# Masked softmax of a batched matmul: transfers of eight rows to a partition over four batches, in buffers of 2 MB

## Chip, cores and metric

One core of a Trainium2 chip. The metric is the time of one execution on the device in microseconds (us); lower is better. The kernel before takes 91.02 us (median of 3 runs, 90.93 to 91.16). Faster or slower means by over 2%.

## The reference

```python
batch, m, k, n = 16, 512, 512, 512            # x: (16, 512, 512), weight: (512, 512), float32
y = scale * np.matmul(x, weight)              # scale = 0.125
y = np.where(mask == 1, y, -1e9)              # mask: 1 strictly below the diagonal
y_exp = np.exp(y - np.max(y, axis=-1, keepdims=True))
return (y_exp / np.sum(y_exp, axis=-1, keepdims=True)).astype(np.float32)
```

16.8 MB come in as x, 16.8 MB go out. Row 0 of each batch is fully masked and becomes 1/512.

## The kernel before

Work goes in 16 units of 1 MB. A unit is one half of the rows (`h`) of two neighbouring batches: partition `2p + e` holds rows `4p` to `4p + 3` of that half of batch `e`, which are 8 KB in one run of memory. For the upper half only 256 columns are computed. The mask's diagonal blocks are turned into an additive `band`, which one extra matmul adds. All transfers go through one queue.

```python
X_BUFS = 8
OUT_BUFS = 8
T = 4
x_r = x.rearrange("(c e) (h p t) k -> c h p e (t k)", e=2, h=2, t=T)
out_r = out.rearrange("(c e) (h p t) n -> c h p e (t n)", e=2, h=2, t=T)
# ... cut: tiles
def load(u):
    xf = x_pool.tile([P, T, K], FP32, name="xf")
    seq(nc.sync.dma_start(xf.rearrange("p t k -> p (t k)"), x_r[u // 2, u % 2]))
# ... cut: cast (DVE), transpose (PE), evict (DVE and ACT), multiply (PE, exp on ACT), normalise (DVE)
load(0)
seq(nc.sync.dma_start(w_f32, weight.rearrange("(p kt) n -> p kt n", kt=KT)))
load(1)
seq(nc.sync.dma_start(diag_f32, diag_r))      # four 128 x 128 blocks of the mask, 512-byte pieces
for u in range(2, X_BUFS):
    load(u)
# ... cut: clears, spins that keep PE's clock up, first two units, band
for u in range(U + 1):
    if 2 <= u + 1 < U:
        transpose(u + 1)
    if u + 2 < U:
        cast(u + 2)
    if 2 <= u + 1 < U:
        evict(u + 1)
    if u < U:
        multiply(u)
    if u >= 1:
        normalise(u - 1)
        store(u - 1)
        if u - 1 + X_BUFS < U:
            load(u - 1 + X_BUFS)
```

The softmax here doesn't subtract the row's maximum and nothing guards it: scores larger than these inputs give would overflow.

## Time and profile before

| | before |
|---|---|
| time, span in the profile | 91.02 us, 89.1 us |
| DMA share of the queue | 94.2% |
| last store issued / landed | 80.1 / 88.05 us |
| PE busy | 74.3 us, ends at 77.3 us |

### The profile page before, as it was taken

Reading aid. Unit: us, or ns where it says so; the run is one execution under the profiler, and the core shown is the slowest. Engines: PE = TensorE matmul, PEld = TensorE weight load, DVE = VectorE, ACT = ScalarE, POOL = GpSimd, SP = SyncE. Lnnn points to the kernel's source line nnn. Section 1 sums busy time; section 2 is a strip of 40 time slices with the busy share of each in tenths; the row PEclk is TensorE's granted clock in tenths of the full one; section 3 lists DMA queues with packets and bytes.
Section 4 is the critical chain, followed back from the end, with each engine's and each line's share of the span. In section 5 each row is a group of like instructions: output and inputs, shape, how many; then the busy total and the mean of one; then the engine's idle time right before and its main releaser. Section 6 shows DMA issues by size and latency. Waiting matters only on the chain.

```text
span 89.1 us, 1666 instructions
## 1 busy us (share of the span) xinstructions
PE 74.3 (83%) x616; PEld 50.0 (56%) x616; DVE 60.3 (68%) x123; ACT 55.0 (62%) x154; POOL 7.3 (8%) x20
## 2 busy tenths in 40 slices
PE   4967979899999999999999999999999999700000
PEld 1315454685795598579659847964984784300000
DVE  5876263989499779949977977967494999080000
ACT  5402604977697686969768786977778796710000
POOL 7620000002001000200100020002000102000000
PEclk9999999999999999999999999999999999995555
DMA  1899779999999999999999999999999999999970
GB/s 22 313 408 431 293 289 438 419 431 419 427 419 431 419 431 419 416 419 431 423 427 412 434 427 423 423 431 423 419 416 445 416 427 419 434 419 427 434 316 33
DMA packets 5287, 34.97 MB, mean 393 GB/s; under 512 B 544, under 2 KB 1056, under 8 KB 1056
## 3 DMA queue, kind: packets, MB, share of 16 engines
q1 hardware_dynamic: 5280, 34.87, 94.2%
q8 instruction: 5, 0.08, 0.3%
q14 instruction: 2, 0.02, 0.0%
HBM read 18.09 MB, written 16.78 MB: 392 GB/s over the span
## 4 chain that ended last, share of the span: by engine, by line
PE 72%; DMA 10%; DVE 4%; SPq 1%; ACT 1%; DVEq 0%; issue 0%; ACTq 0%
PE py L117 47%; PE pt L93 15%; DMA xf<-in_x_dram 10%; PE py L126 8%; PE py L175 2%; DVE ot L153 1%; DVE xb L84 1%; SPq L79 1%; ACT ot L136 1%; SPq L163 1%; DVE band L226 0%; DVEq L272 0%; ACT band L226 0%; PE py L219 0%; DVE rinv L151 0%
## 5 line engine op out<-in xcount | busy, mean ns | idle before, releaser
L117 PE MATMUL py<-w_bf,xt 128*128 128x256 bf16 (+1 forms) x256 | 49.4, 326 | 0.3 <-ACT band L226 0.3
L136 ACT ACTIVATE ot<-py 128x256 f32<-128x256 f32 (+1 forms) x64 | 31.2, 493 | 7.3 <-PE py L126 7.1
L117 PEld LDWEIGHTS <-xt 128*128 128x128 bf16 x256 | 24.4, 98 | 12.6 <-issue 0.5
L104 ACT COPY xt<-pt 128x1024 bf16<-128x1024 bf16 x16 | 16.2, 1012 | 13.6 <-PE pt L93 9.4
L84 DVE CAST xb<-xf 128x2048 bf16<-128x2048 f32 x16 | 19.5, 1220 | 7.2 <-DMA xf<-in_x_dram 7.2
L153 DVE TENSOR_SCALAR ot<-ot,rinv 128x256 f32<-128x256 f32 (+1 forms) x64 | 23.5, 431 | 0.8
L93 PE MATMUL pt<-ident_bf,xb 128*128 128x128 bf16 x256 | 17.0, 219 | 1.7 <-DVE xb L84 1.7
L93 PEld LDWEIGHTS <-xb 128*128 128x128 bf16 x256 | 15.9, 114 | 3.6 <-DVE xb L84 2.7
L126 PE MATMUL py<-band,ident_bf 128*128 128x256 bf16 x64 | 17.4, 273 | 0.0
L103 DVE COPY xt<-pt 128x1024 bf16<-128x1024 bf16 x16 | 11.0, 686 | 6.4 <-PE pt L93 6.4
L136 ACT ACTIVATION_READ_ACCUMULATOR ot<-py 128x1 f32 x64 | 12.8, 200 | 0.0
L175 PE MATMUL py<-zeros 128*128 128x512 bf16 x36 | 10.3, 447 | 1.2 <-DVE zeros L170 1.2
L155 POOL MEMSET ot<- 2x256 f32 x8 | 3.6, 449 | 65.8 <-DVE ot L153 65.8
L126 PEld LDWEIGHTS <-ident_bf 128*128 128x128 bf16 x64 | 6.3, 98 | 4.1
L175 PEld LDWEIGHTS <-zeros 128*128 128x128 bf16 x36 | 3.9, 112 | 6.3 <-issue 2.7
L151 DVE RECIPROCAL rinv<-rsum 128x4 f32<-128x4 f32 x16 | 2.7, 168 | 2.6 <-ACT ot L136 2.6
L183 DVE MEMSET ot<- 128x1024 f32 x4 | 3.6, 912 | 0.6 <-issue 0.6
L226 DVE CAST band<-py 64x256 bf16<-64x256 f32 x4 | 1.4, 408 | 1.4 <-PE py L219 1.4
L226 ACT CAST band<-py 64x256 bf16<-64x256 f32 x4 | 1.4, 367 | 1.4 <-DVE band L226 1.4
L190 ACT ACT_TABLE_LOAD x1 | 1.3, 1283 | 0.7 <-PEq L258 0.7
L184 POOL MEMSET ot<- 2x256 f32 x4 | 1.2, 301 | 1.5 <-DVE ot L183 1.4
L190 ACT COPY spread<-ident_bf 128x128 bf16<-128x128 bf16 x4 | 1.0, 330 | 0.2 <-POOL ident_bf masks.py:199 0.2
(14 smaller groups left out, 6.7 us busy)
## 6 DMA issues: line engine op xcount, KB each, us to landing
xf<-in_x_dram SPq DMA_DIRECT2D x16, 1024.0 KB, 14.9
out_dram<-ot SPq DMA_DIRECT2D x16, 1024.0 KB, 12.1
w_f<-in_weight_dram SPq DMA_DIRECT2D x1, 1024.0 KB, 7.0
diag_f<-in_mask_dram SPq DMA_DIRECT2D x1, 256.0 KB, 10.5
```

The source lines that it names most:

```text
L84: seq(nc.vector.tensor_copy(xb, st_x.pop(u)))
L93: nc.tensor.transpose(st_pt[u][kt // 2][:, kt % 2, t], xb[:, t].rearrange("p (k kt) -> p kt k", kt=KT)[:, kt], ident_bf,)
L103: seq(nc.vector.tensor_copy(xt[:, 0:2], pt[0]))
L104: seq(nc.scalar.copy(xt[:, 2:4], pt[1]))
L117: nc.tensor.matmul(py[:, :NC], lhsT=xt[:, kt, t], rhs=w_bf[:, kt, :NC], start=(kt == 0), stop=(kt == KT - 1),)
L126: nc.tensor.matmul(py[:, h * HB : NC], lhsT=ident_bf, rhs=band[:, h, t], start=False, stop=True, skip_group_check=True,)
L136: nc.scalar.activation(out=ot[:, t, :NC], in_=py[:, :NC], func=AF.Exp, bias=0.0, scale=float(scale), accum_out=rsum[:, t : t + 1],)
L153: seq(nc.vector.tensor_scalar_mul(ot[:, t, :NC], ot[:, t, :NC], rinv[:, t : t + 1]))
L155: seq(nc.gpsimd.memset(ot[0:2, 0, :HB], 1.0 / N))
L175: seq(nc.tensor.matmul(idle, lhsT=zeros[:, :P], rhs=zeros, start=True, stop=True))
L183: nc.vector.memset(ots[i][:, :, HB:], 0.0)
L226: seq(copy(band[half, :, t, g * P : (g + 1) * P], src[half, :, g]))
```

## The change

The intent: longer runs, so fewer packets, and fewer and larger transfers. A transfer now covers half the rows of four batches, with eight rows (16 KB) to a partition, 2 MB in all. It holds two units. The first load and the last store stay halved. Five load buffers and four output buffers of 2 MB replace eight and eight of 1 MB. A position in a partition now stands for one of eight rows, so the band has eight slots.

```diff
-X_BUFS = 8
-OUT_BUFS = 8
+X_BUFS = 5
+OUT_BUFS = 4
...
-    xb_pool = ctx.enter_context(tc.tile_pool(name="xb", bufs=3))
-    xt_pool = ctx.enter_context(tc.tile_pool(name="xt", bufs=3))
+    xb_pool = ctx.enter_context(tc.tile_pool(name="xb", bufs=2))
+    xt_pool = ctx.enter_context(tc.tile_pool(name="xt", bufs=2))
...
-    x_r = x.rearrange("(c e) (h p t) k -> c h p e (t k)", e=2, h=2, t=T)
+    x_r = x.rearrange("(c e) (h p t) k -> c h p e (t k)", e=E, h=2, t=S)   # E = 4, S = 8
...
-    band = const.tile([P, 2, T, HB], BF16, name="band")
-    ots = [const.tile([P, T, N], FP32, name=f"ot{i}") for i in range(OUT_BUFS)]
+    band = const.tile([P, 2, S, HB], BF16, name="band")
+    ots = [const.tile([P, S, N], FP32, name=f"ot{i}") for i in range(OUT_BUFS)]
...
-    for t in range(T):
+    for t in range(S):
         pm = psum_y.tile([P, N], FP32, name="py")
...
             normalise(u - 1)
-            store(u - 1)
-            if u - 1 + X_BUFS < U:
-                load(u - 1 + X_BUFS)
+            g, second = divmod(u - 1, 2)
+            if g == G - 1:
+                store(g, slots(u - 1))
+            elif second:
+                store(g)
+                if g + X_BUFS < G:
+                    load(g + X_BUFS)
```

Look at the end: a store and the load behind it used to be issued for each unit, so the queue turned from stores to loads and back in steps of 1 MB. Now the steps are 2 MB.

More of the change, by code (lines that the diff above doesn't have):

```diff
@@ L43 @@
     K2, N = weight.shape
-    assert K == K2 and N == 512 and K == 512 and M == 512 and B % 2 == 0
+    assert K == K2 and N == 512 and K == 512 and M == 512 and B % 4 == 0
     KT = K // P
+    E = 4
+    S = 8
     T = 4
@@ L48 @@
     HB = 2 * P
-    U = B
+    G = B // 2
+    U = 2 * G
     const = ctx.enter_context(tc.tile_pool(name="const", bufs=1))
     x_pool = ctx.enter_context(tc.tile_pool(name="xf", bufs=X_BUFS))
-    xb_pool = ctx.enter_context(tc.tile_pool(name="xb", bufs=3))
-    xt_pool = ctx.enter_context(tc.tile_pool(name="xt", bufs=3))
+    xb_pool = ctx.enter_context(tc.tile_pool(name="xb", bufs=2))
+    xt_pool = ctx.enter_context(tc.tile_pool(name="xt", bufs=2))
     sum_pool = ctx.enter_context(tc.tile_pool(name="sums", bufs=4))
@@ L57 @@
     psum_y = ctx.enter_context(tc.tile_pool(name="psum_y", bufs=4, space=bass.MemoryType.PSUM))
-    x_r = x.rearrange("(c e) (h p t) k -> c h p e (t k)", e=2, h=2, t=T)
-    out_r = out.rearrange("(c e) (h p t) n -> c h p e (t n)", e=2, h=2, t=T)
+    x_r = x.rearrange("(c e) (h p t) k -> c h p e (t k)", e=E, h=2, t=S)
+    out_r = out.rearrange("(c e) (h p t) n -> c h p e (t n)", e=E, h=2, t=S)
     diag_r = bass.AP(tensor=mask.tensor, offset=mask.offset, ap=[[N, P], [P * N + P, KT], [1, P]])
@@ L68, with slots, load @@
     diag_bf = const.tile([P, KT, P], BF16, name="diag_bf")
-    spread = const.tile([P, T, P], BF16, name="spread")
+    spread = const.tile([P, S, P], BF16, name="spread")
     zeros = const.tile([P, N], BF16, name="zeros")
-    band = const.tile([P, 2, T, HB], BF16, name="band")
-    ots = [const.tile([P, T, N], FP32, name=f"ot{i}") for i in range(OUT_BUFS)]
+    band = const.tile([P, 2, S, HB], BF16, name="band")
+    ots = [const.tile([P, S, N], FP32, name=f"ot{i}") for i in range(OUT_BUFS)]
     st_x, st_xb, st_pt, st_xt, st_sum = {}, {}, {}, {}, {}
     seq = tc.keep_in_program_order
-    def load(u):
-        xf = x_pool.tile([P, T, K], FP32, name="xf")
-        seq(nc.sync.dma_start(xf.rearrange("p t k -> p (t k)"), x_r[u // 2, u % 2]))
-        st_x[u] = xf
+    def slots(u):
+        return slice(T * (u % 2), T * (u % 2) + T)
+    def load(g, part=slice(0, S)):
+        if g not in st_x:
+            st_x[g] = x_pool.tile([P, S, K], FP32, name="xf")
+        run = slice(part.start * K, part.stop * K)
+        seq(nc.sync.dma_start(st_x[g].rearrange("p t k -> p (t k)")[:, run], x_r[g // 2, g % 2][:, :, run]))
     def cast(u):
         xb = xb_pool.tile([P, T, K], BF16, name="xb")
-        seq(nc.vector.tensor_copy(xb, st_x.pop(u)))
+        seq(nc.vector.tensor_copy(xb, st_x[u // 2][:, slots(u)]))
         st_xb[u] = xb
@@ L107, in multiply @@
     def multiply(u):
-        h = u % 2
+        h = u // 2 % 2
         NC = (h + 1) * HB
         xt = st_xt.pop(u)
-        ot = ots[u % OUT_BUFS]
+        ot = ots[u // 2 % OUT_BUFS][:, slots(u)]
         rsum = sum_pool.tile([P, T], FP32, name="rsum")
@@ L128, in multiply @@
                     lhsT=ident_bf,
-                    rhs=band[:, h, t],
+                    rhs=band[:, h, slots(u)][:, t],
                     start=False,
@@ L147, in normalise @@
     def normalise(u):
-        ot = ots[u % OUT_BUFS]
-        NC = (u % 2 + 1) * HB
+        ot = ots[u // 2 % OUT_BUFS][:, slots(u)]
+        NC = (u // 2 % 2 + 1) * HB
         rinv = sum_pool.tile([P, T], FP32, name="rinv")
@@ L153, in normalise, with store @@
             seq(nc.vector.tensor_scalar_mul(ot[:, t, :NC], ot[:, t, :NC], rinv[:, t : t + 1]))
-        if u % 2 == 0:
-            seq(nc.gpsimd.memset(ot[0:2, 0, :HB], 1.0 / N))
-    def store(u):
-        ot = ots[u % OUT_BUFS]
-        seq(nc.sync.dma_start(out_r[u // 2, u % 2], ot.rearrange("p t n -> p (t n)")))
-    load(0)
+        if u % 4 == 0:
+            seq(nc.gpsimd.memset(ot[0:E, 0, :HB], 1.0 / N))
+    def store(g, part=slice(0, S)):
+        ot = ots[g % OUT_BUFS]
+        run = slice(part.start * N, part.stop * N)
+        seq(nc.sync.dma_start(out_r[g // 2, g % 2][:, :, run], ot.rearrange("p t n -> p (t n)")[:, run]))
+    load(0, slots(0))
     seq(nc.sync.dma_start(w_f32, weight.rearrange("(p kt) n -> p kt n", kt=KT)))
-    load(1)
+    load(0, slots(1))
     seq(nc.sync.dma_start(diag_f32, diag_r))
-    for u in range(2, X_BUFS):
-        load(u)
+    for g in range(1, X_BUFS):
+        load(g)
     nc.vector.memset(zeros, 0.0)
@@ L183 @@
         nc.vector.memset(ots[i][:, :, HB:], 0.0)
-        nc.gpsimd.memset(ots[i][0:2, 0, HB:], 1.0 / N)
+        nc.gpsimd.memset(ots[i][0:E, 0, HB:], 1.0 / N)
     for g in range(2):
-        for e in range(2):
+        for e in range(E):
             seq(
                 nc.scalar.copy(
-                    spread.rearrange("k t (g p e) -> k t g p e", g=2, e=2)[:, :, g, :, e],
-                    ident_bf.rearrange("k (p t) -> k t p", t=T),
+                    spread.rearrange("k t (g p e) -> k t g p e", g=2, e=E)[:, :, g, :, e],
+                    ident_bf.rearrange("k (p t) -> k t p", t=S),
                 )
```

## The prediction

> **What bounds the kernel now.** I read the page's chain first, then the DMA slices, then time stretches, because chain and slices disagree.
>
> The chain that ended last, from the page of the kernel before:
>
> ```profile
> PE 72%; DMA 10%; DVE 4%; SPq 1%; ACT 1%; DVEq 0%; issue 0%; ACTq 0%
> ```
>
> This looks like a TensorE bound. But here are the slices (each 89.1 / 40 = 2.23 us) and the queue totals of that page:
>
> ```profile
> PE   4967979899999999999999999999999999700000
> ...
> DMA  1899779999999999999999999999999999999970
> GB/s 22 313 408 431 293 289 438 419 431 419 427 419 431 419 431 419 416 419 431 423 427 412 434 427 423 423 431 423 419 416 445 416 427 419 434 419 427 434 316 33
> ...
> q1 hardware_dynamic: 5280, 34.87, 94.2%
> ```
>
> PE is busy from about 16 us on but has nothing left in the last five slices. The DMA engines are full from the seventh slice to the 38th, three slices after PE has ended. Stretches cut at the events show it (columns: stretch, length, busy time of PE, PEld, DVE, ACT, POOL, PE clock, DMA share, GB/s):
>
> ```profile
> 10.00:12.50 2.50, 2.03 (x13) 0.83 (x11) 1.23 (x1) 0.33 (x1) 0.00 (x0) 1.00 0.62 181
> 12.50:76.00 63.50, 63.24 (x566) 45.15 (x564) 50.77 (x109) 49.21 (x142) 3.59 (x8) 1.00 1.01 425
> 76.00:80.00 4.00, 1.44 (x8) 0.57 (x6) 1.76 (x5) 1.60 (x6) 0.00 (x0) 1.00 1.03 428
> 80.00:85.00 5.00, 0.00 (x0) 0.00 (x0) 0.09 (x1) 0.00 (x0) 0.00 (x0) 0.54 1.01 428
> ```
>
> So from 12.5 to 85 us the engines move 425 to 428 GB/s without a hole; the one hole (10 to 12.5 us) is the mask diagonal in 512-byte pieces. The queue's own waits agree:
>
> ```profile
> SPq L159 <- DVE ot L153: 56.0, 16, 12.4
> SPq L272 <- DMA out_dram<-ot: 7.3, 1, 7.3
> ```
>
> The issuer waits for results before it issues a store (line 1), yet the engines stay full behind it, because earlier issues are still queued. At the end everything waits 7.3 us for the last store (line 2). That store is issued at 80.1 us. Its engines finish the store before it between 83.2 and 85.6 us, so it stands in a queue, and lands by 88.05 us. I conclude: the time is the data divided by the DMA rate, plus a fixed head and tail; PE is second, with 1.7 us (fastest DMA engine) to 4.1 us (slowest) to spare. I get that from the first load, which took 1.43 us from issue (0.74) to first packet (2.17): 80.1 + 1.43 = 81.5, against 83.2 and 85.6.
>
> **What the Trainium skill says.**
> "DMA: Bandwidth & Descriptors", Where 436 GB/s comes from: the ports set a ceiling of 435.2 GB/s. The trace runs at 425, so at most 2.4% is there to win from any packet shape.
> Same page, Why small descriptors are slow: a fixed cost of about three cycles for each packet. The packet records of this trace agree in kind: median 309 ns for 8192 bytes, 27 ns for 512 bytes. A line through both gives 282 ns / 7680 B = 0.0367 ns a byte (27.2 GB/s an engine, 436 on 16, the ceiling again) plus 8.2 ns a packet.
> Same page, Queues, rings and completion order: each DMA engine takes its descriptors in ring order. The trace agrees: landings come in issue order. I use this for the schedule below.
> Same page, Latency and other measured facts: row pitches of 2 MiB and more slow copies down (512 KiB did little). The four batches here are 1 MB apart (two batches before, also 1 MB); all-load and all-store stretches both show 309 ns, so this trace has no sign of it.
>
> **The change, part by part.**
>
> *Packets (path).* Before, 33 one-megabyte transfers (16 loads, 16 stores, the weights) make 33 x 128 = 4224 packets of 8 KB. After, seven loads and seven stores of 2 MB make 14 x 128 = 1792 packets of 16 KB; the first load and last store stay halved, 4 x 128 = 512 packets of 8 KB, and the weights 128. So 1792 pairs of 8 KB become single packets: 112 on each of 16 engines, each saving 8.2 ns: 0.92 us. A 16 KB packet should take 8.2 + 16384 x 0.0367 = 610 ns against 618. The instruction fetches, the only 16 KB packets in this trace, took 934 to 1046 ns, about one 8 KB packet (309) more than 610, which fits their taking turns with one. DMAs fall from 34 to 20, so 14 completion writes (9 ns) an engine go: 0.13 us at most, and they seem to run beside data (share 1.01), so I count 0.05. Sum: about -0.95 us on the path that sets the end. Rate: 425 to about 430 GB/s.
>
> *Band build (PE start).* The additive mask now has eight slots, not four. Its eviction before:
>
> ```profile
> L226 DVE CAST band<-py x4: 405/406/416, 15.3 to 16.3; 64x256 bf16<-64x256 f32 x4
> L226 ACT CAST band<-py x4: 367/367/367, 15.8 to 16.8; 64x256 bf16<-64x256 f32 x4
> ```
>
> Starts lie 0.33 us apart on both engines. Four more take 4 x 0.34 = 1.35 us on each, side by side. There are four accumulation buffers, so the first multiply, which began at 16.19 after the first ACT eviction, now gets its buffer after the fifth: about 1.35 us later, 17.5. PE has no slack of its own from there to 77.3 us in the chain (eight pairs of 3.09 and 4.77 us, less the two transposes done earlier, are 61.1 us = 77.3 - 16.2), so PE ends near 78.7 and the last store is issued near 81.45. Needed at the DMA engines: 83.2 to 85.6 less the 0.9 saved, 82.3 to 84.7; there at 81.45 + 1.43 = 82.9. The fastest engine may idle 0.6 us, the slowest, which sets the end, has 1.8 us left. Cost on the path: 0.
>
> *Larger loads (PE feed).* Unit 2 used to land alone at 15.7 us; now units 2 and 3 land together near 18. The cast of unit 2 was at 16.66 us; it now stands behind the eight band casts until 18.1 anyway. PE multiplies unit 0 until 19.7, so it does not notice. Later pairs land near 23, 28 and 33 and are used at 28, 36 and 44. The last three loads wait for stores: issued near 28, 36 and 42, landed near 42, 52 and 62 by ring order, transposed at 51, 59 and 67. Cost 0.
>
> *Stores in pairs (queue depth).* The first store goes from 21.5 to about 27.5 us. But five loads of 2 MB fill the queue until about 33 us. Walking on at 4.9 us per 2 MB, each store is issued 3 to 12 us before the queue would run dry; the tightest are the last full store (ready 73.3, needed 76) and the two final halves (77.6 against 81; 81.45 above). Cost 0, unless I misjudge one by 3 us.
>
> *Buffers.* Four 2 MB output buffers hold what eight of 1 MB held. The fourth is written again by unit 14 from about 72 us; its store lands near 67 to 68. Casts and transposed tiles in two buffers, not three: in program order each buffer's reader on PE precedes its next writer, so no new wait.
>
> *Off the path.* Four more spread copies on ACT (4 x 330 ns at 3 us, ACT idle then), clears twice as long but half as many on DVE (same 3.6 us), fewer small POOL clears.
>
> Sum: 91.02 - 0.95 + about 0.05 for small frictions = 90.1.
>
> **Rivals.**
> *16 KB packets win nothing* (split internally into what 8 KB was, or the 8 ns overlaps in long packets): 91.0. For it: 309 against 27 ns is a line through two points, and small packets may pay what large ones hide. Against: the slope lands on the port ceiling.
> *The queue runs dry between 2 MB stores, or PE starves on a late pair*: each miss costs up to a store's delay, 1 to 3 us, so 91.5 to 93. For it: PE and DMA are within 2 to 4 us of each other at the end, and the issuer waits 56 us for DVE. Against: the walk above, and the totals buffered are larger than before for loads (10 MB against 8).
> *The PE chain sets the end*: if the head grows 3.2 us or more rather than 1.35, the last store starts late. 2 us beyond my estimate gives about 90.3, 4 us gives 92.3. Speaks for it: the head is a serial DVE-ACT-PE relay. Against: its durations are read, not guessed.
> *Four interleaved batches conflict in memory*: 5% of the rate would be 4 us, 94. Nothing in the trace speaks for it[...].
>
> **Range and chances.** The gain has a ceiling: at 435 GB/s the whole stream would save 2.3% of some 84 us, 1.9 us, so faster by over 2% (below 89.2) would need nearly all of it. The losses are larger but need a misjudged wait. Uneven DMA engines (they end 2.4 us apart now, in part through instruction fetches) move the end some tenths either way. So 90.1, range 89.4 to 91.2; faster 0.05, same 0.88, slower 0.07.
>
> **What would show it.** Right: 16 KB packets near 610 ns; 428 to 431 GB/s in the full stretches; no DMA hole between 12.5 us and the end; first multiply near 17.5 us, PE ending near 78.7, no PE wait for a cast after that start; last store issued near 81.4; 3264 queue packets (1792 of 16 KB, 640 of 8 KB, 512 of the mask, 16 completion writes for each of 20 DMAs) against 5280. Wrong: 618 ns for 16 KB, a DMA slice below 9 after 13 us, PE idle behind a cast, or a last store whose landing follows its issue by less than 5.2 us, the unqueued time of the first load, which would mean that the compute chain set the end.

## More of the kernel before

The prediction shows the slices and stretches that make this a DMA-bound kernel. Three further stretches of the kernel before serve for comparison: loads only, loads and stores mixed, and mostly stores (columns: stretch, length, busy time and instructions of PE, PEld, DVE, ACT, POOL, PE clock, DMA share, GB/s).

```profile
12.50:36.00 23.50, 23.24 (x214) 16.69 (x212) 18.82 (x38) 17.20 (x50) 0.90 (x2) 1.00 1.01 425
36.00:64.00 28.00, 28.00 (x255) 20.09 (x253) 21.85 (x47) 22.41 (x64) 1.80 (x4) 1.00 1.01 424
64.00:80.00 16.00, 13.44 (x108) 8.95 (x105) 11.87 (x30) 11.20 (x35) 0.89 (x2) 1.00 1.01 426
```

The last column is what to read: the rate is the same whether the queue loads, mixes or stores.

## The result, and the profile after

The changed kernel takes 91.15 us (91.10 to 91.41, 4 runs) against 91.02: ratio 1.0018, interval 0.9995 to 1.0042. Run again beside other kernels on two occasions it was 91.45 against 90.99 (ratio 1.0050, 1.0035 to 1.0066) and 91.40 against 90.93 (1.0045, 1.0024 to 1.0066). So it is "same", and on the wrong side: 0.2 to 0.5% slower, where 1.0% faster was predicted. A ratio is the mean time of one kernel's fast runs over that of the other's of the same rounds, so it is not quite the ratio of the medians quoted.

The slices, the queue totals and the queue's waits of the changed kernel:

```profile
PE   4977979899999999999999999999999999930000
...
DMA  0999799999999999999999999999999999999950
GB/s 11 349 393 426 286 343 434 426 434 434 426 426 426 441 434 419 423 419 423 411 434 434 419 419 441 426 397 441 426 404 441 441 411 441 426 411 419 423 231 15
...
q1 hardware_dynamic: 3264, 34.87, 93.4%
```

```profile
SPq L168 <- DVE ot L161: 67.9, 9, 21.4
SPq L285 <- DMA out_dram<-ot: 6.1, 1, 6.1
```

Almost every sign that the prediction named for "right" is there; the rate where loads and stores mix is not (below). There are 3264 packets, as counted. The DMA row has no hole after the mask stage. The 16 KB packets have a median of 611 ns in the packet records (610 predicted). The band build is as worked out, and the first multiply starts at 17.53 us (17.5 predicted):

```profile
L235 DVE CAST band<-py x8: 402/404/417, 15.3 to 17.7; 64x256 bf16<-64x256 f32 x8
L235 ACT CAST band<-py x8: 367/367/368, 15.8 to 18.1; 64x256 bf16<-64x256 f32 x8
```

The last store is issued at 81.5 us (81.4 predicted) and lands at 88.10 us, 6.6 us later. That is longer than the 5.2 us of a load with no queue ahead, so by the prediction's own test the compute chain does not set the end. Yet the landing is 88.10 us against 88.05 before. The stretches show where the gain is and where it is missing:

```profile
12.50:36.00 23.50, 23.24 (x207) 16.23 (x205) 18.79 (x40) 17.92 (x53) 0.45 (x1) 1.00 1.00 428
36.00:64.00 28.00, 28.00 (x249) 19.67 (x247) 22.51 (x50) 21.94 (x64) 0.90 (x2) 1.00 1.01 425
64.00:80.00 16.00, 14.78 (x128) 10.23 (x125) 10.66 (x27) 12.31 (x37) 0.45 (x1) 1.00 1.01 428
80.00:85.00 5.00, 0.00 (x0) 0.00 (x0) 1.43 (x4) 0.00 (x0) 0.00 (x0) 0.92 0.97 413
```

Line 1 (loads) and line 3 (stores) run 3 and 2 GB/s above the kernel before. Line 2 (mixed) does not: 425 here, 423 and 422 in the two later traces of this kernel, 424 before; the prediction wanted 428 to 431. Line 4 is easily misread. It looks as if engines idle from 80 to 85 us (0.97), but the view counts a packet in the stretch in which it starts. With the packet records cut at the bounds, the engines are 101% busy until 85 us, as before.

A transfer lands when all 16 engines have written their part, and the trace records each of the 16. For the last store:

| trace | first engine | mean of 16 | last engine | spread |
|---|---|---|---|---|
| before | 85.68 | 86.96 | 88.05 | 2.38 us |
| after | 85.61 | 86.52 | 88.10 | 2.50 us |

The mean engine came in 0.44 us earlier. The last one did not, and the program waits for the last one. So the question becomes: why did the slowest engine not gain?

**How engines come apart.** With the packets of each engine linked end to start, three things put engines behind. The 512-byte mask stage leaves them 0.4 to 1.4 us apart, where it stands between the first loads. Then each block of instructions is fetched through one of the same engines, 16 KB at a time. In the trace of before the first is at 20.8 us: the spread of landings (first engine to last) goes from 1.09 us (19.5 us) to 2.32 us (22.0 us), so one engine falls 1.2 us behind. There are five such fetches in the span:

```profile
q8 instruction: 5, 0.08, 0.3%
```

A refill is a packet of 8 KB from one more queue (q14 in the traces): it takes 0.31 us on one engine in most cases, and the data packet behind it runs another 0.2 to 0.65 us longer than usual. And the lag stays while the queue is full: in the two traces of the kernel before the spread is 2.2 to 2.5 us from 24 us to the end. That is all in the kernel before. The kernel after has a further thing: single packets that take 0.2 to 0.8 us longer than others of their size with no fetch near. I count these *stray stalls*: packets between 36 and 64 us (where loads and stores mix) that took over 150 ns more than the usual 309 or 611 ns and did not start within 40 ns of the end of a fetch or refill. The trace of before has none. The trace of after has eight, 3.7 us in sum. In it the last engine falls from 1.34 us behind the mean (store landing from 36.5 us) to 1.98 us behind (load from 41.3 us). Stray stalls are not confined to late engines: in this trace three hit engines behind the mean, among them the last, and five hit engines ahead of it. Only stalls of late engines can move the end.

### The profile page after: what moved, and what is told of

The parts are those of the page before. It is cut to its first block, busy times and chain, and to the rows that moved or that the text cites. A ratio compares the mean times of both kernels' runs of the same rounds, so it can differ in the third digit from the quotient of the medians.

```text
span 89.2 us, 1649 instructions
## 1 busy us (share of the span) xinstructions
PE 75.7 (85%) x620; PEld 50.4 (57%) x620; DVE 61.0 (68%) x125; ACT 58.1 (65%) x162; POOL 6.6 (7%) x14
## 3 DMA queue, kind: packets, MB, share of 16 engines
q1 hardware_dynamic: 3264, 34.87, 93.4%
## 4 chain that ended last, share of the span: by engine, by line
PE 74%; DMA 10%; DVE 4%; SPq 1%; ACT 1%; DVEq 0%; issue 0%; ACTq 0%
PE py L125 47%; PE pt L101 15%; DMA xf<-in_x_dram 10%; PE py L134 8%; PE py L184 2%; PE py L228 2%; DVE ot L161 1%; DVE xb L92 1%; SPq L88 1%; ACT ot L144 1%; SPq L172 1%; DVE band L235 0%; DVEq L285 0%; ACT band L235 0%; DVE rinv L159 0%
## 5 line engine op out<-in xcount | busy, mean ns | idle before, releaser
L161 DVE TENSOR_SCALAR ot<-ot,rinv 128x256 f32<-128x256 f32 (+1 forms) x64 | 23.0, 423 | 0.7
L92 DVE CAST xb<-xf 128x2048 bf16<-128x2048 f32 x16 | 19.5, 1221 | 5.7 <-DMA xf<-in_x_dram 5.7
L163 POOL MEMSET ot<- 4x256 f32 x4 | 1.8, 449 | 62.6 <-DVE ot L161 62.6
L192 DVE MEMSET ot<- 128x2048 f32 x2 | 3.5, 1765 | 0.7 <-issue 0.7
L235 DVE CAST band<-py 64x256 bf16<-64x256 f32 x8 | 2.7, 406 | 1.4 <-PE py L228 1.4
L235 ACT CAST band<-py 64x256 bf16<-64x256 f32 x8 | 2.7, 367 | 1.4 <-DVE band L235 1.4
L199 ACT COPY spread<-ident_bf 128x128 bf16<-128x128 bf16 x8 | 2.7, 476 | 1.0 <-POOL ident_bf masks.py:199 1.0
L228 PE MATMUL py<-diag_bf,spread 128*128 128x512 bf16 x8 | 2.4, 378 | 0.3 <-ACT band L235 0.3
L190 POOL MEMSET band<- 64x2048 bf16 x1 | 1.8, 1801 | 0.1
```

Source lines behind the costliest of these rows:

```text
L92: seq(nc.vector.tensor_copy(xb, st_x[u // 2][:, slots(u)]))
L161: seq(nc.vector.tensor_scalar_mul(ot[:, t, :NC], ot[:, t, :NC], rinv[:, t : t + 1]))
L192: nc.vector.memset(ots[i][:, :, HB:], 0.0)
L228: nc.tensor.matmul(pm, lhsT=spread[:, t], rhs=diag_bf.rearrange("k b c -> k (b c)"), start=True, stop=True)
L235: seq(copy(band[half, :, t, g * P : (g + 1) * P], src[half, :, g]))
```

## The experiments

**Lag theory:** the slowest DMA engine sets the end; longer packets help all engines, and stray stalls in the mixed stage take the gain from the late ones, whichever others they also hit. **Rivals:** the compute chain, started 1.35 us later, sets the end; or 16 KB packets gain nothing. Within the lag theory it is open whether packet size, row layout or the 2 MB turns make the stalls. The landing records of all traces, with times, are in the table after the last run.

### The changed kernel again

No edit.

> The changed kernel again, for a second trace and a finer ratio. Lag theory (the slowest of the 16 DMA engines ends the kernel; the others gained 0.4 to 0.6 us from the longer packets, but the slowest lost it to lag): 91.1 to 91.3 us, 0 to 0.3 us behind the kernel before; last store landing spread over 2.3 to 2.6 us between first and last engine, mean of the 16 near 86.5 us. If the lag of the changed kernel was chance in one trace, this trace will have its slowest engine nearer 87.7 and a time near 90.6.

91.45 us. Mean 86.45, last 88.43, spread 3.12 us; nine stray stalls. The gain of the mean engine repeats, and so does the loss of the last. Here engines left the mask stage only 0.5 us apart, and the spread still grew to 3.1: to 1.9 by the first fetch, then by steps near 41 us and 61 us. So the lag was not chance in one trace. The time is 0.15 us above the range expected.

### 8 KB packets in the changed kernel

```diff
-        seq(nc.sync.dma_start(st_x[g]...[:, run], x_r[g // 2, g % 2][:, :, run]))
+        for lo in range(run.start, run.stop, T * K):
+            piece = slice(lo, lo + T * K)
+            seq(nc.sync.dma_start(st_x[g]...[:, piece], x_r[g // 2, g % 2][:, :, piece]))
```
and the same for stores.

> The changed kernel with every 2 MB transfer cut into two 1 MB halves issued back to back, so packets are 8 KB as before; bands, buffers and order stay. Lag theory: the 16 KB packets are worth about 5 ns a pair (two 306 ns steps against one 607 ns step), 112 pairs an engine, so the mean engine ends 0.45 to 0.65 us later than in the changed kernel; time 91.5 to 91.8 if the lag stays as it is. Rival (16 KB packets win nothing on the path): 91.1 to 91.3, the same as the changed kernel. Rival (16 KB packets make the stalls near 40 and 59 us): the slowest engine loses no lag there and the time is about 91.0.

91.44 us, mean 87.09 us, spread 2.80 us; four stray stalls. The mean engine is 0.6 us later than in the three traces with 16 KB packets (86.45 to 86.52), which was the expectation: the packets are worth that. The time, against expectation, is that of the changed kernel of the same rounds (91.45): the first rival's number came out, though its reason did not, since the mean engine lost 0.6 us and the spread was smaller here (2.80 against 3.12). The second rival's number, 91.0, did not come, but stalls are fewer; the later runs take that up.

### Less compute

```diff
-            for kt in range(KT):
+            for kt in range(1):
...
-                        stop=(kt == KT - 1),
+                        stop=True,
```
Only in `multiply`; the result is wrong.

> The changed kernel with only one of the four products of each multiply (wrong result on purpose): TensorE ends over 10 us earlier. Lag theory: DMA-bound, 91.0 to 91.3 us within 0.3 us of the changed kernel, perhaps some tenths less since TensorE then has 384 instructions of its 1240 fewer, so about 3 instruction fetches in place of 5. Rival (the compute chain, started 1.35 us later by the longer band build, sets the end): at least 1 us faster, below 90.2.

91.38 us. In this run PE is done before 76 us, and the DMA engines are not:

```profile
76.00:80.00 4.00, 0.00 (x0) 0.00 (x0) 1.35 (x4) 0.00 (x0) 0.00 (x0) 0.50 1.03 442
80.00:85.00 5.00, 0.00 (x0) 0.00 (x0) 0.00 (x0) 0.00 (x0) 0.00 (x0) 0.50 0.96 408
```

DVE's last work falls before 80 us too, and the time stays (91.38 against 91.45 of the changed kernel in the same rounds). The compute-chain rival is out. The fetches fell as expected:

```profile
q8 instruction: 3, 0.05, 0.2%
```

Three fetches in place of five still left a spread of 2.60, with twelve stray stalls.

### The mask diagonal on another queue

```diff
-    seq(nc.sync.dma_start(diag_f32, diag_r))
+    seq(nc.scalar.dma_start(diag_f32, diag_r))
```

> The changed kernel with the mask diagonal (512-byte pieces) issued from the Activation queue beside the first loads in place of between them. Lag theory: the hole at 10 to 12.5 us (about 0.6 us a mean engine) and the 1.0 us of lag that engines bring out of it both shrink, so the end comes 0.6 to 1.6 us earlier: 89.6 to 90.6 us. Rival (compute chain sets the end): no more than 0.3 us, 90.9 to 91.2. If lag comes from instruction fetches alone: 0.5 us, 90.6.

93.31 us: a miss, 1.86 us slower than the changed kernel of the same rounds. The diagonal now came first and held up the first load:

```profile
8.88 1.23 DVE L92 CAST xb<-xf 128x2048 bf16<-128x2048 f32 x1 [3.46 <-DMA xf<-in_x_dram]
10.16 1.89 PE L101 MATMUL pt<-ident_bf,xb 128*128 128x128 bf16 x16 [4.76 <-DVE xb L92]
```

PE sat idle 4.8 us and its clock fell to half (0.50 from 8 to 12 us in the stretches). The first multiply began at 21.8 us, 4.2 us later than in the changed kernel, and the last store was issued at 85.7 us. It landed at 90.8, with its engines only 1.0 us apart: here the compute chain did set the end. The last store took 5.1 us from issue to landing, where it takes 6.6 and 7.2 us in the first two traces of the changed kernel, so there the chain has some 1.5 to 2.1 us to spare; the prediction said 1.8. The end says nothing of the lag, but stray stalls are frequent in this trace: 43 between 36 and 64 us.

### The kernel before again

> The kernel before once more, for a second trace of it and as the scale of noise. Ratio 1.00. Lag theory: first to last landing of the last store spread over 2.3 to 2.5 us as in its first trace, mean of the 16 near 86.95 us, and no stalls of pairs of engines between 36 and 64 us. If those stalls are mere chance, this trace has some too and its spread is 2.5 to 3.1.

90.89 us, mean 86.92, last 88.19, spread 2.19 us; no stray stalls.

### Two-batch rows in the changed order

Rows, runs and band as before (`E = 2`, four rows, 8 KB), but two halves loaded and stored together:

```diff
-    x_r = x.rearrange("(c e) (h p t) k -> c h p e (t k)", e=E, h=2, t=S)
+    x_r = x.rearrange("(c j e) (h p t) k -> c h j p e (t k)", j=2, e=E, h=2, t=T)
...
+        for j in range(part.start // T, part.stop // T):
+            seq(nc.sync.dma_start(st_x[g]...[:, j], x_r[g // 2, g % 2, j]))
```

> The changed kernel's order and buffers (two halves loaded together, two stored together), but the rows as before: two batches to a transfer, four rows to a partition, 8 KB runs, four band slots. Beside the version with the four-batch rows in 8 KB packets (91.44 us, spread 2.80, mean 87.10). If the four-batch row layout makes the stalls: spread near 2.4, 90.9 to 91.1 us. If the paired order (5 MB of loads and stores turning in 2 MB steps) makes them: spread 2.6 to 3.1, 91.3 to 91.6. Mean engine 86.9 to 87.1 in both. If the longer band build counts: a last store issued 1.3 us earlier would show as 0.4 us or more.

91.95 us, ratio 1.0106 (1.0092 to 1.0121), above the range expected of either. Mean 87.26, spread 2.81, last landing 89.09; ten stray stalls. This kernel has the packets and rows of the kernel before and only the changed order, with its buffers, and it is 1% slower. The row layout and the longer band are not needed for the stalls. What is left is the order or the buffers; the runs in turns of 1 MB below keep these buffers and have no stalls.

### Only loads, only stores in 8 KB

The edit of the 8 KB version, for one direction.

> The changed kernel with only the loads cut into 8 KB halves; stores stay 16 KB. Packet part of the lag theory: half of the gain goes, so the mean engine ends near 86.8 us, midway between 86.5 and 87.1. Time 91.1 to 91.5 whatever it does, since the spread of 2.5 to 3.1 sets it. If 16 KB loads make the stalls: fewer stalls over 150 ns between 36 and 64 us than the changed kernel's 9 to 15, and a time at or under 91.1.

91.59 us, mean 86.86, spread 2.78; eight stray stalls.

> The changed kernel with only the stores cut into 8 KB halves; loads stay 16 KB. Mean engine again near 86.8 us, time 91.1 to 91.5. If 16 KB stores make the stalls: fewer stalls than the changed kernel's and a time at or under 91.1.

91.31 us, mean 86.73, spread 2.78; twelve stray stalls. Each direction gives about half of the packet gain to the mean engine, and neither stops the stalls; nor did 8 KB in both: packet size is not their cause.

### 16 KB packets in turns of 1 MB

The changed kernel, each store and later load cut into even and odd partitions (64 partitions by 16 KB), issued in turn:

```diff
             elif second:
-                store(g)
-                if g + X_BUFS < G:
-                    load(g + X_BUFS)
+                for j in range(2):
+                    rows = ots[g % OUT_BUFS].rearrange("(q j) t n -> q j (t n)", j=2)[:, j]
+                    seq(nc.sync.dma_start(out_e[g // 2, g % 2, j], rows))
+                    if g + X_BUFS < G:
+                        n = g + X_BUFS
+                        if n not in st_x:
+                            st_x[n] = x_pool.tile([P, S, K], FP32, name="xf")
+                        rows = st_x[n].rearrange("(q j) t k -> q j (t k)", j=2)[:, j]
+                        seq(nc.sync.dma_start(rows, x_e[n // 2, n % 2, j]))
```
with `x_e` and `out_e` as `x_r`, its four batches split as `e=2, j=2`.

> The changed kernel with its stores and later loads cut by partition parity into 1 MB transfers of 64 partitions by 16 KB, and store and load taken in turn: packets stay 16 KB, the turns are 1 MB as in the kernel before. If the 2 MB turns make the stalls of the late engines: stalls over 150 ns between 36 and 64 us (fetches aside) fall to nearly none, spread 2.1 to 2.5, mean 86.5, last landing 87.6 to 87.9, time 90.4 to 90.7, better than both kernels. Rival (late engines stall whatever the turns, because 16 KB packets or five deep loads make them): spread 2.5 to 3.1, time 91.1 to 91.5. If 64 partitions feed the engines badly: much slower, above 93.

90.53 us against 90.93 before in the same rounds: ratio 0.9955 (0.9936 to 0.9974). No stray stalls; mean 86.36, last 87.82, spread 2.29. It beats both kernels, by 0.4 us and by 0.9 us. The mixed stretch, first of the changed kernel run in the same rounds, then of this one:

```profile
36.00:64.00 28.00, 27.79 (x246) 19.67 (x248) 22.27 (x50) 21.91 (x63) 0.90 (x2) 1.00 1.00 422
```

```profile
36.00:64.00 28.00, 27.79 (x245) 19.67 (x247) 23.18 (x50) 21.91 (x63) 0.90 (x2) 1.00 1.01 428
```

The compute columns are the same to a few hundredths but for DVE; the rate is higher by 6 GB/s. (With packets cut at the bounds of the stretch it is 425 against 422, still below the 428 of the loads.) The edit also halves the partitions of a transfer, which the next run does not.

### 8 KB packets in turns of 1 MB

```diff
-            if g == G - 1:
-                store(g, slots(u - 1))
-            elif second:
-                store(g)
-                if g + X_BUFS < G:
-                    load(g + X_BUFS)
+            store(g, slots(u - 1))
+            if g + X_BUFS < G:
+                load(g + X_BUFS, slots(u - 1))
```

> The changed kernel with 8 KB packets and the old turns: each unit stored as soon as it is done and followed by the load of one half. If the 2 MB turns make the stalls: spread 2.1 to 2.5, mean 86.9 to 87.1, time 90.8 to 91.1, as the kernel before. If the four-batch rows or the longer band build cost something on the path: 91.3 to 91.6 as with paired 8 KB halves (91.44).

90.75 us, ratio 0.9984 (0.9962 to 1.0005). No stray stalls; mean 86.99. One thing the edit leaves: the four full loads at the start are still 2 MB in 16 KB packets.

```profile
q1 hardware_dynamic: 4704, 34.87, 94.2%
...
xf<-in_x_dram SPq DMA_DIRECT2D x4, 2048.0 KB, 21.5
```

That is 32 pairs of 8 KB packets less on each engine than in the kernel before, worth some 0.16 us at 5 ns a pair. So with turns and most packets undone, what is left of the change (rows, band, buffers) costs 0.2 us at most. This trace's last store found idle engines and spread over only 1.38 us; the spread of the store before it is 2.10.

### The changed kernel a third time

> The changed kernel a third time, as the partner of the next two on the same chip. Mean of the last 16 landings 86.4 to 86.6 us, spread 2.5 to 3.1 us, time 91.1 to 91.5.

91.40 us, mean 86.45, last 88.31, spread 2.89; eight stray stalls.

### No mask diagonal to load

```diff
-    seq(nc.sync.dma_start(diag_f32, diag_r))
+    nc.gpsimd.memset(diag_f32, 1.0)
+    # for each block: affine_select keeps 1 where row > column, else 0
```

> The changed kernel with the diagonal of the mask made on the chip and not loaded (right for this mask only): no 512-byte pieces. Lag theory: the stream loses about 0.9 us of data and a hole of 0.6 us, so the mean engine ends 1.2 to 1.5 us earlier (85.0 to 85.3), and the 0.5 to 1.1 us of lag that engines bring out of that stage go too, so the slowest ends 1.5 to 2.5 us earlier: time 89.0 to 89.7. If the lag at the end has nothing to do with that stage: 89.8 to 90.1. If the compute chain becomes the bound (last store issued at 81.4): the last store takes less than 5.5 us from issue to landing and the time stays at or above 89.5.

90.92 us, 0.5 us faster than the changed kernel beside it, not 1.5 to 2.4. Two things went otherwise. Nearly all engines stalled together for one or two packets:

```profile
27.50:30.00 2.50, 2.50 (x26) 1.68 (x25) 1.82 (x5) 2.05 (x4) 0.00 (x0) 1.00 0.92 216
```

216 GB/s in 2.5 us, half the rate, about 1.2 us lost, in a stretch of loads alone. And the spread still grew, to 3.13 us at the last store but one, through a fetch and seven stray stalls. So the lag that engines bring out of the mask stage is not needed for a large spread. What made all engines stall at once is open; the run with the diagonal on another queue has such places too, and it is not known whether they have to do with the stray stalls.

### All traces side by side

Landing of the last store in us; times in us; stray stalls as defined above.

| kernel | turns | packets | mean | last | stray stalls | time |
|---|---|---|---|---|---|---|
| before, two traces | 1 MB | 8 KB | 86.96, 86.92 | 88.05, 88.19 | 0, 0 | 91.02, 90.89 |
| 8 KB, 1 MB turns | 1 MB | 8 KB, first loads 16 KB | 86.99 | 87.91 | 0 | 90.75 |
| 16 KB, 1 MB turns | 1 MB | 16 KB | 86.36 | 87.82 | 0 | 90.53 |
| after, three traces | 2 MB | 16 KB | 86.52, 86.45, 86.45 | 88.10, 88.43, 88.31 | 8, 9, 8 | 91.15, 91.45, 91.40 |
| less compute | 2 MB | 16 KB | 86.32 | 88.14 | 12 | 91.38 |
| loads in 8 KB | 2 MB | both | 86.86 | 88.67 | 8 | 91.59 |
| stores in 8 KB | 2 MB | both | 86.73 | 88.49 | 12 | 91.31 |
| all in 8 KB | 2 MB | 8 KB | 87.09 | 88.61 | 4 | 91.44 |
| two-batch rows | 2 MB | 8 KB | 87.26 | 89.09 | 10 | 91.95 |

Left out are the diagonal on another queue (43 stray stalls, the chain sets the end) and no diagonal (7), both with 2 MB turns. Read it by columns. The mean follows the packets: 16 KB is about 0.6 us ahead of 8 KB in either kind of turns. The last engine and the stalls follow the turns: every trace with 1 MB turns has none and ends by 88.19, every one with 2 MB turns of 8 KB packets ends at 88.6 or later, and with 16 KB packets the gain and the loss about cancel.

## Why the prediction was wrong

Point by point, by its own steps:

- **What bounds the kernel:** right. Taking 20 of PE's 75.7 us of work away left the time; the chain has 1.5 to 2.1 us to spare (1.8 said). One reading was loose: a landing is recorded some 0.35 us after the engine's last packet, so the 1.7 to 4.1 us of slack before the change were about 1.4 to 3.7.
- **Packets, -0.92 us:** right in kind, too large. In the packet records the next packet of an engine starts 3 ns before the end of an 8 KB packet and 4 ns before the end of a 16 KB one, so the steps are 306 and 607 ns: 5 ns a pair, not 8.2, and 112 x 5 = 0.56 us. The means agree (0.6 us). The 8.2 came from a line through the durations of 512-byte and 8 KB packets. The 8 KB and 16 KB durations alone give 2 x 309 - 611 = 7 ns, and the overlap takes 2 more. The first rival named this ("small packets may pay what large ones hide"), and it was part of the truth. Even so, the last engine got only half of it: with 1 MB turns 16 KB packets won 0.6 us for the mean engine, 0.3 us at the last landing (87.82 against 88.05 and 88.19) and 0.4 us of time.
- **Band build, larger loads, buffers, off the path, cost 0:** right to about 0.2 us. Undoing the turns and most of the packets left 90.75 us against 90.93.
- **"Stores in pairs (queue depth)", cost 0:** this is the step that failed. It asked whether the queue runs dry. It does not. But turning the queue in 2 MB steps makes single engines stall in the mixed stage, late ones among them: two-batch rows in paired order cost 1.0 us against the kernel before with the same packets. With 16 KB packets, going back to 1 MB turns won 0.9 us (91.40 to 90.53). The last landings of the traces show 0.5 us of that (88.31 to 87.82); the rest the traces do not show.
- **"Uneven DMA engines move the end some tenths either way":** here the mistake has its root. The prediction treated the unevenness as noise and the 16 engines as one pipe. The end is the slowest engine's, and the change moved the slowest and the mean in opposite senses: over the traces of both kernels the mean engine came 0.5 us earlier and the last 0.2 us later.
- **Rivals:** "16 KB packets win nothing" fits the time and is wrong; the table shows a win that is given back.

Sum as it turned out, in the rounds that hold all three kernels: -0.4 us for packets (90.93 to 90.53) and +0.9 us for turns (90.53 to 91.40), together +0.5. Over all rounds +0.1 to +0.5 was measured. With 8 KB packets the turns cost about +0.5 (91.44 against 90.75, of other rounds, less some 0.2 for the first loads) or +1.0 (two-batch rows).

Not settled: why engines stall when turns are 2 MB and not when they are 1 MB. The runs exclude packet size, row layout and buffers, and taking work from PE did not lower the count (12). They show the turns as the cause in both directions, but not what in the memory or the queue makes the stall.

## What to carry to other kernels

When the DMA queue is full from end to end, look at the 16 engines one by one: the program waits for the slowest, and a gain on the mean may never reach it. Longer runs and the order in which loads and stores alternate are two changes, so test them apart: here long runs helped and long turns hurt, and keeping 16 KB runs in 1 MB turns beat both kernels. Take the fixed cost of a packet from the step between packets that follow each other, not from the durations of small ones.

## What the Trainium skill lacked or had wrong

- "DMA: Bandwidth & Descriptors", Why small descriptors are slow: the fixed cost of about three cycles a packet comes with no figure for large ones. At 8 to 16 KB the step between packets leaves 5 ns a packet (2 x 306 - 607), and packets overlap by 3 to 4 ns.
- "DMA: Bandwidth & Descriptors", Rules for kernel authors, asks for 1 MiB or more per transfer. It has no word on turns: 2 MB turns of loads and stores against 1 MB turns cost 0.9 us of 91 with 16 KB packets, and about 0.5 to 1.0 us with 8 KB.
- "Runtime: NRT & Kernel Launch", Instruction fetch mechanics, has the 16 KiB blocks of 256 instructions and calls the cost mostly hidden. The trace agrees on the blocks (16 KB each; five fetches with 1240 PE instructions, three with 856). It is not hidden from the data: each fetch takes about 1 us on one of the 16 DMA engines, and in the trace of before the first put its engine 1.2 us behind the next to last, until the second put another there; the last engine is 1.1 to 1.6 us behind the mean from then to the end.
- No page says how far the engines come apart in a full queue, or that they stay so: 2.1 to 3.1 us between the first and the last of 16 in the store before the last here.
- No page explains the common stall of nearly all engines in loads alone (216 GB/s for 2.5 us in the run without the diagonal).
